# A mixer block on one core: keys and queries in unsplit float32, decay masks on TensorE, gates of both sequences together, and a new order of u, z and Fourier

## The chip, the core and the metric

The program runs on one core of one Trainium2 chip. A core has TensorE (PE; its weight loads are shown as PEld), VectorE (DVE), ScalarE (ACT), GpSimd (POOL) and SyncE (SP), which run side by side; every engine takes its own instructions in the order in which they were written for it. The metric is the device time of the whole program in microseconds; lower is better.

## The reference, cut to what matters

A latent of 256 positions by 1024 channels (`x`) and a context of 256 positions (`ctx`) go through a first block, the mixer, and then through recurrent and feed-forward blocks that the change does not touch. In the first block both sequences are modulated and normalised, projected with `w_in`, and mixed by a gated delta rule in both directions and by a 2-D DFT:

```
p = h @ w_in                                # u 512 | q 512, k 512, v 512 | z 512 | ab 16
qkv = silu(dwconv1d(qkv, conv))             # three taps over positions
q, k = l2norm per head (4 heads of 128)
beta = sigmoid(ab[0:2]);  g = -exp(a_log) * softplus(ab[2:4] + dt_bias)   # 2 directions x 4 heads
gc = cumsum(g);  decay = exp(gc_i - gc_j) where i >= j, else 0
a_mat = strict_lower((k*beta) k^T * decay);  T = inverse(I + a_mat)
S <- S * exp(g_last) + k_dec^T v_new;  o = q_dec S + (q k^T * decay) v_new
y = concat(fourier_mix(u, w_f), rmsnorm(o) * silu(z)) @ w_out
```

The context (called sequence 1 in the kernel) gives only keys, values and gates; its final states start the scan of `x` (sequence 0).

## The kernel before, in words

The change lies in `_block1_mix` and its helpers, the first 275 us of the span. Sequence s has two row tiles t of 128 positions and two directions d.

**Products.** `hT[s]` holds the modulated input, channels on partitions, in float32. A unit of `w_in` (128 x 2048, 1 MB) is loaded by SP into a buffer named raw. For keys and queries both operands are split in a high and a low part in fp32r (`split`: ACT copies the high part, L154, DVE subtracts, L155; names hk, hq, wk), and `cm` (L207) makes 24 fp32r matmuls for one 128 x 256 tile. Values, u and z go through `cmn` and `tmn` (L213, L217): 8 float32 matmuls a tile straight from raw and `hT`, each of which the trace shows as two records. There are 8 key tiles (pk), 4 query tiles (pq), 8 value tiles (pv), and the tiles of u (pu) and z.

**From keys to the inverse.** A key tile goes through the convolution with SiLU (`conv_silu`: L629, L630 and L637 on ACT, L633 to L638 on DVE), is transposed (tk, into kn) and squared (L762). Where all squares are there, POOL takes the power -1/2 (rs, L132) and DVE makes the scalars of `gdn_scalars`. A decay tile is made by `decay`: four small matmuls bring the cumulated gate to PSUM (gr, L941), four DVE instructions subtract the column's own and add a mask of 0 and large negative numbers (L946), one ACT exponential takes all 512 columns (L948). Its results are named E and atT. `Mall` (L784, DVE, 32 instructions of 128 x 128) multiplies key products (kk, L778), a scalar and E. kk and gr tiles share one pool of four PSUM buffers (`PA`). `invert` then inverts 32 x 32 blocks on DVE: four transposes (invB, L1028), a row recurrence (L1038, L1040) with the convolutions of queries and values between its steps, four transposes back (Zall, L1044). The merges follow on PE (zt L1114, y and z L1125), interleaved with the scan (ks, tv, up).

**Work around it.** `fill_step` runs one of 24 dot products on DVE (L258, of 128 x 1024 each) for a modulation vector that later blocks use; its operand is a half unit of `adaT` that POOL's queue loads (nar, L254) into one of two narrow buffers, after an activation and a product on the conditioning row (crow, L236 and L237). Steps are called in the loop over values, held there by `issue_after` until named instructions have been issued, and in the scan. After the scan's first steps come u, the DFT (`fourier`, f L1162) and z as filling, then the output product (bk). The order on each engine is made by a scheduler from this program order and from its estimates; it is fixed before the run.

Of the kernel before, what the change touches and what calls it, by code (L numbers as in the profile page):

```python
# [65 lines left out]
class Program:  # L66
# [67 lines left out]
    def softplus(self, out, in_, n):  # L134

        nc = self.nc
        T = lambda s: self.sm.tile([128, 16], F32, name=self.nm(s), tag=s, bufs=2)[:, :n]
# [504 lines left out]
    def _block1_mix(self, g):  # L642
# [52 lines left out]
        pow_ = self.pow  # L695
        mods = next(mods)
        self.halves()
        del self.scratch
        for s in seqs:
            for k in range(8):  # L700
                A, sh = mods[s]
                if s == 1 and k % 2:
                    nc.scalar.activation(hT[s][k], hT[s][k], AF.Identity, scale=A[:, k:k + 1], bias=sh[:, k:k + 1])
                else:
                    last = nc.vector.tensor_scalar(out=hT[s][k], in0=hT[s][k], scalar1=A[:, k:k + 1], scalar2=sh[:, k:k + 1], op0=ALU.mult, op1=ALU.add)
# [3 lines left out]
        for s in seqs:  # L709
            next(gates[s])  # L710


        four = lambda z: z.rearrange("p (a b) -> p a b", a=4)
        big = T([128, 4, 1024], "hk", "Mall", F32R)
        parts = {1: [four(big[:, i]) for i in range(4)], 0: [T([128, 4, 256], "hq", f"vb{i // 2}{i % 2}", F32R) for i in range(4)]}
        for s in seqs:
            for i in range(2):
                self.split(parts[s][i], parts[s][2 + i], hT[s].tiles[i])
        hp = {s: (Blocks(parts[s][:2]), Blocks(parts[s][2:])) for s in seqs}
# [4 lines left out]
        def split_unit(u, places):  # L724
            w = self.load(a["w_in"][u])
            with ExitStack() as ctx:
                if u >= 4:
                    ctx.enter_context(tc.issue_after(conv.ins))
                for i in range(2):
                    self.split(places[i], places[2 + i], w[:, i * 1024:(i + 1) * 1024])  # L730
            return Weights(places[:2], 256), Weights(places[2:], 256)

        def room(*tags):
            if len(tags) == 1:
                z = T([128, 4, 1024], "wk", tags[0], F32R)
                return [z[:, i] for i in range(4)]
            return [T([128, 1024], "wk", t, F32R) for t in tags]

# [3 lines left out]
        ssq = {s: self.const.tile([128, 2, 4], F32, name=f"ssq{s}") for s in seqs}  # L742
        for u in range(2):
            w = split_unit(u, room("Zall") if u == 0 else room("atT0", "ut", "atT1", "sz"))
            for s in seqs:
                for m in range(2):
                    h = 2 * u + m
                    ps = self.PB("pk")
                    self.cm(ps, w, hp[s], m)
                    conv = self.conv_silu(ps, h, kT[s][:, h])  # L750
                    if (u, s, m) == (0, 1, 1):
                        self.hold = conv
                        gate = {s: next(gates[s]) for s in seqs}
                        scalars = {s: self.gdn_scalars(gate[s], ssq[s], g, s) for s in seqs}
                        gc = {s: next(scalars[s]) for s in seqs}
# [4 lines left out]
                    for t in range(2):  # L760
                        j = self.sm.tile([128, 128], F32, name=self.nm("j"), tag="j", bufs=2)
                        nc.scalar.activation(j, kn[s][:, t, h], AF.Square, accum_out=ssq[s][:, t, h:h + 1])  # L762
                    if u == 1 and early:
                        i = early.popleft()
                        E[i] = self.decay(gate[1][1], gc[1], i[2], i[1], None)
        sc = {s: next(scalars[s]) for s in seqs}
# [6 lines left out]
        for s in seqs:  # L773
            for t in range(2):
# [4 lines left out]
                for d in range(2):  # L779
                    if (s, t, d) not in E:  # L780
                        E[s, t, d] = self.decay(gate[s][1], gc[s], d, t, atT[t][:, d] if s == 0 else None)
# [1037 lines left out]
```

## Time and profile before

| | |
|---|---|
| median of 3 runs | 1677.18 us (1676.41 to 1681.1) |
| profiled execution | 1681.0 us, span 1679.2 us, mean granted clock 0.982 |
| busy in the span | PE 96%, DVE 74%, ACT 51%, POOL 4% |
| first block | up to about 275 us of the span |

The span is what the trace covers; the profiled execution is the slowest of the runs shown. A granted clock of 1.00 is 2.4 GHz and one of 0.50 is 1.2 GHz.

### The profile page before, as it was taken

What the parts mean: (1) busy time and instruction counts of PE and PEld (TensorE: products, weight loads), DVE (VectorE), ACT (ScalarE), POOL (GpSimd) and SP (SyncE); (2) the same over time, 40 slices, a digit from 0 to 9 for tenths busy, and PEclk for the clock granted to TensorE, in tenths of its full rate; (3) what the DMA queues carried; (4) which work ended last, traced back from release to release, by engine and by line L of the source; (5) the groups of instructions that cost most, each with busy time, mean ns of one, the idle gap of its engine ahead of it and who ended that gap; (6) DMA issues with size and microseconds to landing.
All of it is one profiled execution on the core that took longest, in us unless ns stands there. A gap on an engine that the chain in (4) does not pass through costs nothing.

```text
span 1679.2 us, 28977 instructions
## 1 busy us (share of the span) xinstructions
PE 1609.1 (96%) x11712; PEld 1503.4 (90%) x11712; DVE 1246.1 (74%) x2237; ACT 864.1 (51%) x1452; POOL 68.6 (4%) x103
## 2 busy tenths in 40 slices
PE   7969999999969999999999999899999999999998
PEld 2867988899959999999999999799999999999997
DVE  4899666999988784987678667687848876786554
ACT  4725454555546664644446444466646444464443
POOL 1150100000000000000000000000000000000000
PEclk9989999999989999999999999999999999999999
DMA  9332524566765655465665758656554656657552
GB/s 378 117 121 87 170 72 163 180 245 219 272 213 212 209 176 175 149 247 176 225 226 204 261 209 294 237 203 218 176 179 153 239 176 226 226 195 270 176 188 89
DMA packets 51686, 333.86 MB, mean 199 GB/s; under 512 B 6112, under 2 KB 6496, under 8 KB 14688
## 3 DMA queue, kind: packets, MB, share of 16 engines
q1 hardware_dynamic: 47808, 318.38, 53.5%
q0 software_dynamic: 3744, 13.63, 2.5%
q8 instruction: 92, 1.51, 0.4%
q14 instruction: 42, 0.34, 0.1%
HBM read 330.94 MB, written 1.05 MB: 198 GB/s over the span
## 4 chain that ended last, share of the span: by engine, by line
PE 81%; DVE 7%; DMA 5%; issue 4%; ACT 3%; POOL 1%; SPq 0%; DVEq 0%; POOLq 0%; ACTq 0%
PE pj L207 43%; PE bk L1280 12%; PE pj L226 7%; PE pj L496 3%; PE bk L535 2%; DVE wlo L155 1%; DMA raw<-w_in 1%; PE bk L226 1%; PE pu L217 1%; DMA raw<-adaT 1%; ACT whi L154 1%; DMA row<-row 1%; DMA nar<-ada 1%; PE pk L207 1%; PE y L1125 1%
## 5 line engine op out<-in xcount | busy, mean ns | idle before, releaser
L155 DVE TENSOR_TENSOR wlo<-raw,whi 128x1024 fp32r<-128x1024 f32 x438 | 520.7, 1221 | 278.5 <-ACT whi L154 277.8
L154 ACT ACTIVATE whi<-raw 128x1024 fp32r<-128x1024 f32 x438 | 445.7, 1054 | 459.1 <-PE pj L207 302.3
L207 PE MATMUL pj<-hT,whi 128*128 128x256 f32 x3584 | 473.2, 285 | 5.3 <-ACT gac L1238 3.2
L207 PEld LDWEIGHTS pj<-hT,whi 128*128 128x128 f32 x3584 | 450.0, 192 | 9.7 <-ACT gac L1238 3.6
L207 PE MATMUL pj<-hT,wlo 128*128 128x256 f32 x1792 | 252.0, 283 | 0.0
L207 PEld LDWEIGHTS pj<-hT,wlo 128*128 128x128 f32 x1792 | 231.3, 192 | 0.4 <-issue 0.4
L1280 PE MATMUL bk<-whi,hid 128*128 128x512 f32 x688 | 189.1, 397 | 17.0 <-ACT hid L154 17.0
L1280 PEld LDWEIGHTS bk<-whi,hid 128*128 128x128 f32 x688 | 128.5, 191 | 44.1 <-ACT hid L154 18.8
L258 DVE CUSTOM_DVE_ANT_0 raw<-raw,crow 128x1024 f32<-128x1024 f32 x104 | 125.0, 1219 | 12.1 <-DMA raw<-adaT 12.0
L1280 PE MATMUL bk<-wlo,hid 128*128 128x512 f32 x344 | 107.4, 394 | 0.0
L226 PE MATMUL pj<-whi,hT 128*128 128x256 f32 x640 | 84.5, 285 | 0.0
L226 PEld LDWEIGHTS pj<-whi,hT 128*128 128x128 f32 x640 | 80.0, 192 | 0.3
L1280 PEld LDWEIGHTS bk<-wlo,hid 128*128 128x128 f32 x344 | 65.5, 190 | 14.0
L1296 DVE SCALAR_TENSOR_TENSOR gac<-gin,cols,gac 128x189 f32<-128x189 f32 (+2 forms) x176 | 66.1, 426 | 2.2 <-ACT gac L1238 2.1
L496 PE MATMUL pj<-whi,hT 128*128 128x256 f32 x320 | 65.9, 299 | 0.9 <-POOL hT L440 0.4
L496 PEld LDWEIGHTS pj<-whi,hT 128*128 128x128 f32 x320 | 54.3, 203 | 2.7 <-ACT hT L431 1.4
L372 POOL TENSOR_TENSOR ss<-ss,nhalf 128x1 f32<-128x1 f32 x22 | 13.0, 593 | 813.9 <-DVE ss L371 813.9
L226 PE MATMUL pj<-wlo,hT 128*128 128x256 f32 x320 | 44.9, 283 | 0.0
L496 PE MATMUL pj<-wlo,hT 128*128 128x256 f32 x160 | 43.0, 303 | 0.0
L226 PEld LDWEIGHTS pj<-wlo,hT 128*128 128x128 f32 x320 | 41.3, 192 | 0.0
L154 ACT ACTIVATE hid<-r 128x512 fp32r<-128x512 f32 x32 | 20.1, 629 | 35.3 <-DVE r L1330 35.3
L431 ACT ACTIVATE hT<-tp,sh,A 128x128 fp32r<-128x128 f32 x80 | 30.1, 459 | 12.1 <-PE tp L424 9.3
(432 smaller groups left out, 2292.3 us busy)
## 6 DMA issues: line engine op xcount, KB each, us to landing
raw<-w_in SPq DMA_DIRECT2D x98, 1024.0 KB, 4.9
raw<-mlp_w SPq DMA_DIRECT2D x64, 1024.0 KB, 4.9
raw<-adaT SPq DMA_DIRECT2D x52, 1024.0 KB, 5.0
raw<-w_up SPq DMA_DIRECT2D x22, 1024.0 KB, 4.9
nar<-adaT POOLq DMA_DIRECT2D x24, 512.0 KB, 4.2
raw<-w_out SPq DMA_DIRECT2D x12, 1024.0 KB, 4.9
raw<-w_down SPq DMA_DIRECT2D x11, 1024.0 KB, 4.9
raw<-lru_w_o SPq DMA_DIRECT2D x8, 1024.0 KB, 4.8
```

What stands on the lines that cost most here:

```text
L154: self.nc.scalar.activation(hi, v, AF.Copy)
L155: self.nc.vector.tensor_tensor(out=lo, in0=v, in1=hi.bitcast(F32), op=ALU.subtract)
L207: self.nc.tensor.matmul(ps, lhsT=ww[k][:, m * 128:(m + 1) * 128], rhs=xx[k], start=(i == 0 and k == 0), stop=(i == 2 and k == 7))
L217: self.nc.tensor.matmul(ps, lhsT=x[k][:, t * 128:(t + 1) * 128], rhs=w[:, k, :], start=(k == 0), stop=(k == 7))
L226: self.last_product = self.nc.tensor.matmul(ps, lhsT=xx[k][:, t * 128:(t + 1) * 128], rhs=ww[k], start=(i == 0 and k == 0), stop=(i == 2 a ...
L258: nc.vector.tensor_tensor_reduce(out=r, in0=r, in1=self.crow[vec], scale=0.5, scalar=0.0, op0=ALU.mult, op1=ALU.add, accum_out=out[:, k:k ...
L431: q("a", lambda: nc.scalar.activation(H[0][k][:, tk(t)], ps[t, g][:, j], AF.Identity, scale=A[:, k:k + 1], bias=sh[:, k:k + 1]))
L496: self.nc.tensor.matmul(ps[:, t], lhsT=H[lo][k][:, tk], rhs=ww[k], start=(lo == j == i == 0), stop=(lo == 1 and j == 7))
L535: self.nc.tensor.matmul(place(t, n), lhsT=xx[k][:, t * 128:(t + 1) * 128], rhs=ww[k], start=(i == 0 and k == 0), stop=(i == 2 and k == 7))
L1125: mm = lambda ps, l, r: nc.tensor.matmul(ps, lhsT=l, rhs=r, start=True, stop=True)
L1280: self.last_product = self.nc.tensor.matmul(banks[t][h], lhsT=xx[:, k, t * 128:(t + 1) * 128], rhs=ww[k][:, h * 512:(h + 1) * 512], start= ...
L1296: self.nc.vector.scalar_tensor_tensor(out=acc[:, r, c], in0=gin[:, ri, ci], scalar=w, in1=acc[:, r, c], op0=ALU.mult, op1=ALU.add)
```

## The change

Keys and queries are made by `cmn` in float32 from `hT` and raw, without splits. The gates of both sequences are made at once: 32 matmuls with `hT` as weights and 16 columns, one chain of small instructions of 32 columns, one power of 16 columns on POOL. A new function `masks` makes the masks in fp32r once; `decay` starts each of its ten PSUM tiles with one 128 x 512 matmul that puts the mask there, adds the four gate matmuls, and takes four exponentials of 128 x 128 on ACT with the column's own gate as bias. The scan's filling is now all u, then all z, then the DFT, and `fill_step` is called in the loop of u and z and in the scan, with no hold.

```diff
-        gates = {s: self.gates1(wab, hT[s], g, s) for s in seqs}
+        gates = self.gates1(wab, hT, g)
...
-            w = split_unit(u, room("Zall") if u == 0 else room("atT0", "ut", "atT1", "sz"))
+            w = unit(u)
...
-                    self.cm(ps, w, hp[s], m)
+                    self.cmn(ps, w, hT[s], m)
...
-            w = split_unit(4 + u, room("Zall") if u == 0 else room("ut", "b0", "sz", "b1"))
+            w = unit(4 + u)
...
-                self.cm(ps, w, hp[0], m)
+                self.cmn(ps, w, hT[0], m)
...
                     self.cmn(ps, w, hT[s], m)
-                    if m == 0:
-                        with tc.issue_after(last.ins), tc.issue_after(pow_.ins), tc.issue_after(self.hold.ins):
-                            self.fill_step()
...
-            if n == 1:
-                self.fourier(ut, dft, fw[:, 0:2], fw[:, 2:6])
+            self.fill_step()
+        self.fourier(ut, dft, fw[:, 0:2], fw[:, 2:6])
...
+    def masks(self, g):
...
+        for i, (m, sign) in enumerate(((self.ident, 1.0), (self.mup, 1.0), (self.mup, -1.0), (self.mlo, 1.0))):
+            nc.scalar.activation(z[:, i], m, AF.Copy, scale=sign)
+        self.mask = z
...
         def fill(e, mask, sign):
+            gr = self.PA("gr", (128, 4, 128))
+            nc.tensor.matmul(gr, lhsT=self.mask[:, 0], rhs=self.mask[:, mask:mask + 1].to_broadcast([128, 4, 128]), start=True, stop=False)
             for h in range(4):
-                nc.vector.scalar_tensor_tensor(out=e[:, h], in0=gr[:, h], scalar=gc[:, d, t, h:h + 1], in1=mask,
-                                               op0=ALU.subtract, op1=ALU.add if sign > 0 else ALU.subtract)
-            nc.scalar.activation(e, e, AF.Exp, scale=float(sign))
+                nc.tensor.matmul(gr[:, h], lhsT=gg[:, d, h, s, t:t + 1].to_broadcast([128, 128]),
+                                 rhs=self.U if d == 0 else self.L, start=False, stop=h == 3)
+            for h in range(4):
+                nc.scalar.activation(e[:, h], gr[:, h], AF.Exp, scale=float(sign), bias=gc[sign][:, d, h, s, t:t + 1])
             return e
...
+        for s in (1, 0):
+            for t in range(2):
+                for k in range(8):
+                    nc.tensor.matmul(ps[:, s, t], lhsT=hT[s][k][:, t * 128:(t + 1) * 128], rhs=wab[:, k, :], start=(k == 0), stop=(k == 7))
...
-        self.rsqrt(f8(rs), f8(ssq), 8)
+        self.rsqrt(f16(rs), f16(ssq), 16)
```

The two decay tiles that `decay` made from one PSUM tile before now take one each, so ten tiles where there were eight. The scheduler's order changes at three places that matter. The first is PE at the end of the keys and the start of the queries. Before:

```order
L778 MATMUL kk_933<-kT_380 128x128 x3
L941 MATMUL gr_938<-cst,gg_504 128x128 x4
L207 MATMUL pq_1047<-hq_367,wk_1040 128x256 x4
L207 MATMUL pq_1047<-hq_368,wk_1040 128x256 x4
L207 MATMUL pq_1047<-hq_369,wk_1040 128x256 x4
```

Now, where the new line L921 is the mask's matmul and L923 the gate's four:

```order
L752 MATMUL kk_720<-kT_383 128x128 x3
L921 MATMUL gr_725<-masks 128x512
L923 MATMUL gr_725<-cst,gg 128x128 x4
L213 MATMUL pq_839<-hx_221,raw_837 128x256 x3
L921 MATMUL gr_740<-masks 128x512
L923 MATMUL gr_740<-cst,gg 128x128 x4
L213 MATMUL pq_839<-hx_221,raw_837 128x256
L213 MATMUL pq_839<-hx_222,raw_837 128x256
L921 MATMUL gr_750<-masks 128x512
L923 MATMUL gr_750<-cst,gg 128x128 x4
L752 MATMUL kk_764<-kT_383 128x128 x4
```

Three query matmuls stand ahead of gr_740 now, and ahead of it the buffers are taken by kk_694, kk_707, kk_720 and gr_725. The second place is PE where the inverse ends and the merges begin (zt). Before, the last value tiles are followed by 20 matmuls of u, with two transposes (tv) and the query sums (pqs) between them:

```order
L213 MATMUL pv_1472<-hx_222,raw_1386 128x256 x4
L217 MATMUL pu_2223<-raw_2221,hx_221 128x256
L828 MATMUL tv_1465<-cst,vT_1457 128x128 x2
L217 MATMUL pu_2223<-raw_2221,hx_221 128x256 x3
L217 MATMUL pu_2223<-raw_2221,hx_222 128x256 x3
...
L217 MATMUL pu_2245<-raw_2243,hx_221 128x256 x4
L1114 MATMUL zt_1517<-cst,Zall 128x128 x4
L1114 MATMUL zt_1524<-cst,Zall 128x128 x4
L272 MATMUL adr_1639<-cst,gc_1265 128x128
L1125 MATMUL y_1532<-zT_1522,Mall_906 128x128 x4
```

Now the merges follow the last value tile directly, and everything of u stands behind them:

```order
L213 MATMUL pv_1161<-hx_222,raw_1087 128x256 x4
L1091 MATMUL zt_1206<-cst,Zall 128x128 x4
L1091 MATMUL zt_1213<-cst,Zall 128x128 x4
L217 MATMUL pu_1923<-raw_1921,hx_221 128x256 x2
L799 MATMUL tv_1130<-cst,vT_1122 128x128 x2
L1102 MATMUL y_1221<-zT_1211,Mall_693 128x128 x4
L217 MATMUL pu_1923<-raw_1921,hx_221 128x256
L799 MATMUL tv_1154<-cst,vT_1146 128x128 x2
```

In all, 29 matmuls of u, three tv and the pqs stand between the merges up to the scan's fourth step; the rest of u, then z, then the DFT follow. The third place is DVE right behind the inverse's last transposes. Before:

```order
L1044 STREAM_TRANSPOSE Zall<-invX 32x32x32 x4
L131 TENSOR_SCALAR rq_1513<-pqs 128x8
L268 TENSOR_TENSOR gc_1265<-gc_1265,cols 128x8
L258 ISA nar_1802,sh_1247<-nar_1802,crow_1266 128x1024
L258 ISA sh_1247 128x1
L839 TENSOR_SCALAR qs<-qs 128x8
L1119 COPY zc_1529<-Zall 128x512
```

Now three convolutions of values, the product on the conditioning row and the first dots stand there:

```order
L1021 STREAM_TRANSPOSE Zall<-invX 32x32x32 x4
L633 SCALAR_TENSOR_TENSOR vT_1122<-cvx_1123,cwh,vT_1122 128x255
L633 SCALAR_TENSOR_TENSOR vT_1146<-cvx_1147,cwh,vT_1146 128x255
...
L237 SCALAR_TENSOR_TENSOR crow_1329<-nar_1331,crow_1329 128x1024
...
L258 ISA nar_1334,gc_1328<-nar_1334,crow_1329 128x1024
...
L1096 COPY zc_1218<-Zall 128x512
L258 ISA nar_1335,gc_1328<-nar_1335,crow_1329 128x1024
```

All 24 dots stand behind the inverse now; before, 8 stood ahead of it and 16 behind. On ACT, the activation L236 of the conditioning row moved from the twentieth place to the third, ahead of the squares of the context (L339); on POOL the issues of G, crow and the first half unit of `adaT` moved ahead of the first powers (ss, L132).

## Rows read from the trace of the kernel before

**Rows 1.** Windows by stage: length, busy of five engines, PE clock, DMA share, GB/s.
```profile
38.20:80.00 41.80, 40.44 (x293) 34.27 (x294) 36.17 (x119) 30.22 (x85) 2.69 (x5) 0.96 0.41 144
80.00:104.00 24.00, 14.29 (x93) 13.10 (x91) 21.06 (x90) 7.78 (x20) 18.72 (x27) 0.80 0.19 62
112.80:163.00 50.20, 43.73 (x207) 36.02 (x206) 48.23 (x114) 22.34 (x66) 1.64 (x3) 0.97 0.28 94
163.00:249.00 86.00, 84.80 (x688) 75.78 (x689) 54.42 (x144) 41.81 (x119) 11.22 (x17) 1.00 0.38 124
249.00:274.20 25.20, 24.83 (x153) 22.65 (x153) 10.29 (x24) 6.81 (x13) 0.00 (x0) 1.00 0.24 84
```
**Rows 2.** Timeline of PE: start, length, work, idle before, its releaser.
```profile
39.34 8.75 PE L963 MATMUL ab<-hx,wab 128*16 128x256 f32 x32 [1.17 <-issue]
...
77.10 1.19 PE L207 MATMUL pk<-hq,wk 128*128 128x256 f32 x8
...
90.34 1.67 PE L941 MATMUL gr<-cst,gg 128*128 128x128 f32 x8 [2.15 <-DVE Mall L784]
...
104.01 9.61 PE L207 MATMUL pq<-hq,wk 128*128 128x256 f32 x64 [5.72 <-DVE wk L155]
...
154.40 1.95 PE L837 MATMUL pqs<-ones,sq 128*128 128x1 f32 x16
...
163.07 1.06 PE L1114 MATMUL zt<-cst,Zall 128*128 128x128 f32 x8 [2.30 <-DVE Zall L1044]
```
**Rows 3.** Chain of work that ended last: start, length, work.
```profile
48.10 5.97 PE pk L207 x48
...
249.20 13.81 PE pu L217 x64
```
**Rows 4.** Groups by form, 38 to 113 us: count, busy us, mean ns.
```profile
L946 DVE SCALAR_TENSOR_TENSOR E<-gr,gc,cst 128x128 f32<-128x128 f32 x24 | 7.2, 343 | 0.3 <-PE gr L941 0.3
...
L946 DVE SCALAR_TENSOR_TENSOR atT<-gr,gc,cst 128x128 f32<-128x128 f32 x16 | 4.5, 340 | 0.0
```
**Rows 5.** Timeline of ACT, start of the span and first key tile.
```profile
9.80 0.63 ACT L339 ACTIVATE xn<-in_ctx 128x512 f32<-128x512 f32 x1 [7.21 <-DMA in_ctx<-ctx]
...
32.03 1.06 ACT L236 ACTIVATE nar<-crow 128x1024 f32<-128x1024 f32 x1 [4.25 <-DMA crow<-crow]
...
52.05 0.38 ACT L629 ACTIVATE cvx<-pk 128x256 f32<-128x256 f32 x1 [1.56 <-PE pk L207]
...
57.27 0.30 ACT L762 ACTIVATE j<-kn 128x128 f32<-128x128 f32 x1
```
**Rows 6.** Timeline of POOL, whole first block.
```profile
23.20 0.75 POOL L234 DMA_DIRECT2D crow<-crow  x1
...
80.84 2.58 POOL L132 TENSOR_TENSOR rs<-rq,nhalf 128x8 f32<-128x8 f32 x1 [2.32 <-DVE rq L131]
...
164.84 0.69 POOL L254 DMA_DIRECT2D nar<-adaT  x1
...
209.60 0.53 POOL L254 DMA_DIRECT2D nar<-adaT  x1 [2.84 <-DVE A L258]
```
**Rows 7.** Timeline of DVE: products, the inverse's first and last transposes.
```profile
90.31 2.15 DVE L784 SCALAR_TENSOR_TENSOR Mall<-kk,mc,E 128x128 f32<-128x128 f32 x8
...
112.81 2.17 DVE L1028 STREAM_TRANSPOSE invB<-Mall 32x1024 f32<-32x1024 f32 x1
...
154.12 8.81 DVE L1044 STREAM_TRANSPOSE Zall<-invX 32x1024 f32<-32x1024 f32 x4
```
**Rows 8.** A window at the idle before the queries, as Rows 1.
```profile
102.00:104.00 2.00, 0.00 (x0) 0.00 (x0) 2.00 (x6) 0.45 (x1) 0.77 (x2) 0.50 0.10 13
```
**Rows 9.** Groups by form on DVE, 163 to 249 us: busy, mean ns, idle before.
```profile
L258 DVE CUSTOM_DVE_ANT_0 nar<-nar,crow 128x1024 f32<-128x1024 f32 x16 | 19.6, 1222 | 8.9 <-DMA nar<-adaT 8.7
```
**Rows 10.** Timeline of ACT at the end of the first block.
```profile
278.48 0.60 ACT L368 ACTIVATE xn<-bk 128x512 f32<-128x512 f32 x1 [1.69 <-DVE yg L391]
...
279.57 2.01 ACT L154 ACTIVATE whi<-raw 128x1024 fp32r<-128x1024 f32 x2 [0.41 <-DMA raw<-w_up]
```

More of the change, by code (lines that the diff above doesn't have):

```diff
@@ L694, in _block1_mix @@
         self.after = (first,)
-        pow_ = self.pow
         mods = next(mods)
         self.halves()
+        self.masks(g)
         del self.scratch
@@ L704, in _block1_mix @@
                 else:
-                    last = nc.vector.tensor_scalar(out=hT[s][k], in0=hT[s][k], scalar1=A[:, k:k + 1], scalar2=sh[:, k:k + 1], op0=ALU.mult, op1=ALU.add)
+                    nc.vector.tensor_scalar(out=hT[s][k], in0=hT[s][k], scalar1=A[:, k:k + 1], scalar2=sh[:, k:k + 1], op0=ALU.mult, op1=ALU.add)
         wab = T([128, 8, 16], "wab", "wab")
         nc.sync.dma_start(wab, a["w_ab"])
-        gates = {s: self.gates1(wab, hT[s], g, s) for s in seqs}
[L709 to L719, printed above, removed]
+        gates = self.gates1(wab, hT, g)
+        next(gates)
         def unit(u):
             return self.load(a["w_in"][u]).rearrange("p (k n) -> p k n", k=8)
[L724 to L737, printed above, removed]
         E, early = {}, deque((1, t, d) for t in range(2) for d in range(2))
@@ L748, in _block1_mix @@
                     ps = self.PB("pk")
-                    self.cm(ps, w, hp[s], m)
[L750 to L755, printed above, removed]
+                    self.cmn(ps, w, hT[s], m)
+                    self.conv_silu(ps, h, kT[s][:, h])
+                    if (u, s, m) == (0, 1, 0):
+                        gate = next(gates)
+                        scalars = self.gdn_scalars(gate, ssq, g)
+                        gc = next(scalars)
                     pt = self.pst.tile([128, 2, 128], F32, name=self.nm("tk"), tag="pst")
@@ L761, in _block1_mix @@
                         j = self.sm.tile([128, 128], F32, name=self.nm("j"), tag="j", bufs=2)
-                        nc.scalar.activation(j, kn[s][:, t, h], AF.Square, accum_out=ssq[s][:, t, h:h + 1])
+                        nc.scalar.activation(j, kn[s][:, t, h], AF.Square, accum_out=ssq[:, h, s, t:t + 1])
                     if u == 1 and early:
                         i = early.popleft()
-                        E[i] = self.decay(gate[1][1], gc[1], i[2], i[1], None)
-        sc = {s: next(scalars[s]) for s in seqs}
+                        E[i] = self.decay(gate[1], gc, 1, i[2], i[1], None)
+        sc = next(scalars)
         roots = self.pow
@@ L934, in _block1_mix @@
         self.yT = yT
-    def decay(self, gg, gc, d, t, out):
+    def masks(self, g):
         nc = self.nc
-        gr = self.PA("gr", (128, 4, 128))
-        for h in range(4):
-            nc.tensor.matmul(gr[:, h], lhsT=gg[:, d, t, h:h + 1].to_broadcast([128, 128]),
-                             rhs=self.U if d == 0 else self.L, start=True, stop=True)
+        z = g.tile([128, 4, 128], F32R, name="masks")
+        for i, (m, sign) in enumerate(((self.ident, 1.0), (self.mup, 1.0), (self.mup, -1.0), (self.mlo, 1.0))):
+            nc.scalar.activation(z[:, i], m, AF.Copy, scale=sign)
+        self.mask = z
@@ new lines, in gates1 @@
+        fl = lambda z: z.rearrange("p d h s t -> p (d h s t)")
+        xx = self.sm.tile([128, 8, 4], F32, name="xx", tag="xx", bufs=1)
+        nc.vector.tensor_tensor(out=xx, in0=pc[:, 8:16], in1=self.row8[:, 0:8].unsqueeze(2).to_broadcast([128, 8, 4]), op=ALU.add)
+        nc.scalar.activation(by(beta), pc[:, 0:8], AF.Tanh, scale=0.5)
+        self.softplus(fl(gg), xx.rearrange("p a b -> p (a b)"), 32)
+        nea = self.const.tile([128, 8], F32, name="nea")
+        nc.scalar.activation(nea, self.row8[:, 8:16], AF.Exp)
@@ new lines, in gdn_scalars @@
+        mul(by(kd), by(kd), both)
+        nc.vector.scalar_tensor_tensor(out=nrm, in0=f16(ssq), scalar=EPS, in1=f16(rs), op0=ALU.add, op1=ALU.mult)
+        nc.vector.tensor_copy(by(vs)[:, 0], nrm)
+        nc.vector.tensor_copy(by(vs)[:, 1], by(os_)[:, 1])
+        nc.vector.tensor_copy(by(os_)[:, 1], nrm)
+        nc.vector.tensor_scalar(out=by(ks)[:, 0], in0=by(egc)[:, 0], scalar1=-1.0, scalar2=None, op0=ALU.mult)
+        nc.vector.scalar_tensor_tensor(out=by(ks)[:, 1], in0=by(egc)[:, 1], scalar=-1.0, in1=by(m)[:, 1], op0=ALU.mult, op1=ALU.mult)
```

106 lines of the change are left out of this document (44 added, 62 removed).

## The prediction

> **What bounds the kernel now.** First read are the windows by stage, since the change touches only the first 275 us. From 163 us on TensorE is the bound: it works 84.80 of 86.00 us and then 24.83 of 25.20 [rows 1]. Before that it is not: it lacks 24 - 14.29 = 9.7 us from 80 to 104 and 50.2 - 43.73 = 6.5 us from 112.8 to 163, while DVE is busy 21.06 of 24 and 48.23 of 50.2 [rows 1]. There the chain keys, squares, scalars, Mall, inverse, first merge sets the pace, most of it on DVE. The timeline of PE shows where it surfaces: 2.15 us behind Mall, 5.72 us behind the query weights' split, 2.30 us behind Zall [rows 2]. The block's time is thus T0, the start of the first merge (163.07 us), plus the PE work issued behind it: 274.2 - 163.1 = 111.1 us. A gain ahead of T0 counts only if no PE work crosses from before T0 to behind it.
>
> **The prices of the products.** An fp32r matmul with 256 columns takes 5.97 / 48 = 0.124 us, a float32 one 13.81 / 64 = 0.216 us a record and 0.432 us in all [rows 3]. A tile of 24 fp32r matmuls is 2.99 us, one of 8 float32 matmuls 3.45 us; the change adds 0.47 us a tile, 3.7 us on 8 key tiles and 1.9 us on 4 query tiles. In return all splits of these operands leave ACT and DVE, and with them the wait of 5.72 us.
>
> The Trainium skill ("FP8 and Floating Point Precision", section "TensorE Precision Notes") says that true float32 takes four passes through the array, of which the kernel's three split products leave out one. The trace's ratio, 0.432 / 0.124 = 3.5, is below the four of that sentence.
>
> **The change, step by step, on the clock of the profiled execution.**
>
> *Start.* On ACT the activation of the conditioning row now stands ahead of the context's squares, which start at 9.80 us [rows 5]. Its transfer was used 32.03 - 23.20 = 8.8 us after its issue [rows 5, 6]. The issue moves to the front of POOL's queue, behind the clearing of Zall, where I put it at 4.5 us (an estimate); the activation then ends at about 4.5 + 8.8 + 1.1 = 14.4 us and the squares begin 4.6 us later. ACT has 4.25 us of idle time ahead of that same activation alone [rows 5], so most is absorbed. Bounds 0 and +4.6; I take +1.6, nearer to nothing.
>
> *Gates.* 32 float32 matmuls with 16 columns are 64 records; the nearest row, one column wide, gives 1.95 / 16 = 0.122 us each, 7.8 us; 1.5 us more for the half clock that follows an idle PE (0.50 in the idle window shown) [rows 2, 8]. From 39.34 + 1.6 the gates end at 50.2 us (before: 48.1).
>
> *Keys.* Before, the keys run from 48.1 to 77.10 + 1.19 = 78.3 us [rows 2]: 30.2 us, of which 23.9 products and 6.3 others. After: 64 x 0.432 = 27.6 plus 5.1 of others (one set of gate sums falls away), last key at 82.9 us: +4.6.
>
> *Squares and power.* The first key tile goes from ACT's first touch at 52.05 to its second square at 57.6 us, 5.5 us [rows 5], with splits beside it; 5.3 here. POOL's power took 2.58 us for 8 columns [rows 6] and is 16 wide now: at least the 2.6, at most twice that, 5.2; I take 3.0, as most of it should not grow with columns. Scalars at about 91.2 us. Before, half of the products were already done by then, since each sequence had its own power.
>
> *Mall.* 32 products at 2.06 / 8 = 0.257 us [rows 7] are 8.2 us: 99.4 us if the decay tiles are ready. 24 + 16 subtractions of 0.34 us (11.7 us busy) [rows 4] and the queries' splits have left DVE. But the order shows gr_740 behind three key products and gr_725, and the pool has four buffers: gr_740 waits until Mall has read the first (8 products, 93.3 us). PE waits for Mall in the same way now [rows 2]. PE has then only three query matmuls to do, idles some 4 us, and runs on at half clock [rows 8]. What follows goes link by link: a mask and four gate matmuls (eight records 1.67 us [rows 2], with the mask 1.9), four exponentials at 0.30 us [rows 5], four products at 1.0 us. gr_740, then kk_764, then gr_769 and gr_784 each wait for a link; I count 5.1 us beyond the 8.2 (bounds 0 and +7.6). The inverse starts at 104.5 us, before 112.81 [rows 7]: -8.3.
>
> *Inverse.* From 112.81 to 163.07 it is 50.2 us [rows 2, 7]. A dot (1.15 us), some convolutions and small instructions and a wait of 1 us leave it: 47.0. T0 = 151.5 us, 11.5 earlier. The last value tile ends near 142 us (queries and values together are 12 tiles x 3.45 = 41 us of PE from about 101), and PE idles there for up to 10 us, because the order puts the merges straight behind the values.
>
> *Behind T0.* 20 u matmuls (8.64 us), the pqs (1.95 us [rows 2]) and three tv (0.7) cross from before T0 to behind it: 11.3 us. PE was full there, so all of it is added to the 111.1: 122.4. For the half clock after the idle and for places where the chain of merges has less filling I add 2.5 (bounds 0 and +9): 125 us, block products' end at 276.5, +2.3.
>
> *The block's end.* ACT's second square of the output waits behind two splits of 2.01 us [rows 10]; the new order puts both squares first. Bounds 0 and -2.0; I take -1.4.
>
> **Sum.** -11.5 (T0) + 11.3 (work that crosses) + 2.5 - 1.4 = +0.9 us. The profiled execution takes 1681.0 us for a span of 1679.2, 3.8 above the median of 1677.18; the difference is set on the median: 1678 us, no change that can be measured (0.3%, or 5 us, is about what a measurement of this kernel can tell).
>
> **The rivals.**
>
> *Faster.* The decay tiles do not hold Mall (-5.1) and the start hides its squares (-1.6): 0.9 - 6.7 = -5.8, 1671 us; with nothing lost in the merges as well 1669. For it: ACT does exponentials of 0.30 us quickly, and DVE is free at that time. Against it: four buffers and a fixed PE order; 2.15 us of such a wait stand in the trace already [rows 2]. Chance 0.27.
>
> *Slower.* The dots become a wait. All 24 stand behind the inverse, with two narrow buffers; 15 loads issued from 164.84 to 209.60 us make one each 3.2 us [rows 6], and DVE idled 8.7 us for 16 of them [rows 9]. For 24 this makes 13 us of idle DVE, in which the residuals (r) and states (S) of the scan are queued behind the waiting dot, and PE behind them. Before, PE lost only 1.2 us of 86 [rows 1], since u and the DFT lay between the merges; if two thirds of the 13 us surface, +8: 1686 us. It decides as soon as a load lasts longer than the DVE work between two dots. Chance 0.22.
>
> *Dearer float32.* Were a float32 matmul worth four fp32r ones, 0.498 us in place of 0.432, 64 of them would make the last key 4.2 us later, and T0 and the end with it: 1682 us. The rows at 0.432 are of the same instruction, on the same operands' kinds, so chance 0.05. It is what the four passes of the Trainium skill ("FP8 and Floating Point Precision") would give.
>
> **How the numbers follow.** The forecast holds 0.46, the faster rival 0.27, the slower ones 0.27. The range goes from 1667 (the faster case with its bounds) to 1688 (the dots with a start that is 2 us later); the likeliest case's own range is 1673 to 1682.
>
> **What the profile after would show.** Right, if key and query matmuls are 0.43 us, the last key ends near 83 us, invB starts near 104 with PE idle for Mall ahead of it, zt starts near 151 behind an idle PE of up to 10 us, and the products behind it take 125 us to the output product's first half. Wrong, if invB starts before 100 (the buffers did not hold), if zt to bk is well over 125 us with DVE idle for nar (the dots), if the powers on POOL grow with columns to 5 us, or if the start shows hx later by several us.

## The result and the profile after

The changed kernel takes 1696.26 us (median of 4 runs, 1691.7 to 1700.54) against 1678.61 us for the kernel before: ratio 1.0097, 95% interval 1.0077 to 1.0118. It is slower by about 16 us, which lies outside the predicted range. The profiled execution takes 1697.21 us with a span of 1695.4, 16.2 us above that of before.

First, where the span grew. The chain of work of the changed kernel (start, length, work), from the start to the inverse; `...` marks rows left out:

```profile
5.08 9.72 DMA crow<-crow
14.83 1.06 ACT nar L236
15.88 2.45 ACT xn L339 x8
...
44.34 1.82 PE ab L943 x14
46.16 1.04 PE pk L213 x2
47.20 5.36 PE ab L943 x26
...
56.58 3.65 PE ab L943 x18
60.24 6.65 PE pk L213 x24
...
89.97 2.16 PE pk L213 x10
...
93.87 0.39 ACT cvx L629
...
98.73 2.92 POOL rs L132
...
102.58 2.07 DVE Mall L758 x8
104.69 0.50 PE gr L921
...
111.26 2.16 DVE invB L1005
```

The row's activation stands ahead of the context's squares, which begin at 15.8 us instead of 9.80 [rows 5]; the gates start at 44.34 instead of 39.34 [rows 2], and take until 60.24. Float32 products cost what was predicted, 2.16 / 10 = 0.216 us a record, and the 16 wide power 2.92 us (predicted 3.0). The hold of gr_740 is there too (PE idle for Mall 2.12 us, ahead of 104.69), but the inverse starts only 8.8 us after Mall begins, not 13.3. The timeline of DVE shows why: while gr_740 was made, eight more products were ready, and DVE ran 16 without a gap.

```profile
102.49 4.21 DVE L758 SCALAR_TENSOR_TENSOR Mall<-kk,mc,E 128x128 f32<-128x128 f32 x16
...
108.97 1.12 DVE L758 SCALAR_TENSOR_TENSOR Mall<-kk,mc,atT 128x128 f32<-128x128 f32 x4 [0.21 <-ACT atT L926]
```

The windows of the changed kernel through the gates and the first keys (columns as in [rows 1]):

```profile
44.00:46.00 2.00, 1.66 (x15) 1.69 (x15) 2.00 (x7) 1.71 (x4) 0.00 (x0) 0.95 0.69 291
46.00:48.00 2.00, 2.00 (x9) 1.82 (x9) 1.46 (x5) 0.00 (x0) 0.00 (x0) 0.50 0.00 0
...
58.00:60.00 2.00, 2.00 (x11) 2.00 (x10) 0.00 (x0) 0.00 (x0) 0.00 (x0) 0.50 0.00 0
60.00:62.00 2.00, 2.00 (x7) 1.64 (x7) 1.61 (x12) 0.53 (x3) 0.00 (x0) 0.50 0.00 0
62.00:64.00 2.00, 2.00 (x9) 1.69 (x8) 1.26 (x14) 0.52 (x2) 0.00 (x0) 0.79 0.00 0
```

PE is busy all the time, and yet its clock stays at 0.50 (1.2 GHz) from 46 to 62 us. It rises at about 63 us, in the key products behind the last of the gates. In the kernel before it was low at this place too, but only for some 3 us, behind a PE that had idled, and it rose under the gates themselves:

```profile
38.00:40.00 2.00, 0.83 (x6) 0.41 (x6) 1.54 (x7) 1.21 (x4) 0.00 (x0) 0.91 1.02 430
40.00:42.00 2.00, 2.00 (x6) 0.66 (x5) 2.00 (x7) 2.00 (x5) 0.00 (x0) 0.50 0.87 360
42.00:44.00 2.00, 2.00 (x8) 0.84 (x7) 2.00 (x5) 1.89 (x2) 0.00 (x0) 0.74 0.19 78
44.00:46.00 2.00, 2.00 (x11) 0.88 (x10) 2.00 (x2) 0.89 (x2) 0.00 (x0) 1.00 0.00 0
```

Behind the inverse, the timeline of PE (idle before, and its releaser, in brackets):

```profile
159.42 1.94 PE L1091 MATMUL zt<-cst,Zall 128*128 128x128 f32 x8 [3.52 <-DVE Zall L1021]
...
250.06 0.49 PE L845 MATMUL o<-vx,atT 128*128 128x128 f32 x2 [1.72 <-DVE atT L837]
...
253.87 6.49 PE L217 MATMUL pu<-raw,hx 128*128 128x256 f32 x21 [2.03 <-DVE sz L874]
```

and the timelines of ACT and DVE there:

```profile
246.29 2.00 ACT L154 ACTIVATE wm<-raw 128x1024 fp32r<-128x1024 f32 x2 [6.50 <-DMA raw<-w_out]
```
```profile
247.38 2.36 DVE L155 TENSOR_TENSOR wm<-raw,wm 128x1024 fp32r<-128x1024 f32 x2 [2.61 <-ACT wm L154]
249.66 0.35 DVE L837 SCALAR_TENSOR_TENSOR atT<-qk,rs,atT 128x128 f32<-128x128 f32 x1
249.92 1.22 DVE L258 CUSTOM_DVE_ANT_0 nar<-nar,crow 128x1024 f32<-128x1024 f32 x1
...
251.06 1.22 DVE L258 CUSTOM_DVE_ANT_0 nar<-nar,crow 128x1024 f32<-128x1024 f32 x1
...
252.21 1.28 DVE L847 TENSOR_TENSOR os<-o,os 128x512 f32<-128x512 f32 x2
253.41 0.74 DVE L874 SCALAR_TENSOR_TENSOR sz<-sz,pu 128x256 f32<-128x256 f32 x2
```

The first merge starts at 159.42, only 3.7 us before that of [rows 2]. From there to the second half of the output product (first L226 matmul, 274.23 before, 290.80 now) it is 131.4 us instead of 111.2. Of the 20.2 us more, 12.1 are work, 4.5 clock loss and 3.6 idle time. Two waits make most of the 5.1 us that PE idles there now. It waits 1.72 us for the last atT, which stands behind the output weights' split: u, which comes later, holds its buffer longer, so that load is issued at 239.4 us instead of 205.0, and ACT's split waits 6.50 us for it. It then waits 2.03 us for sz, which stands on DVE behind two dots and os.

One count serves all that follows. From the gates' first matmul to the output product's second half, in windows of 2 us, the last one cut short, PE's idle time is the length less its busy time, its clock loss is busy time times (1 - granted clock), and the rest is work at full clock. Before: 234.9 us = 18.0 idle + 8.0 clock + 208.9 work. After: 246.5 = 15.1 + 13.0 + 218.4. With 5.0 us from the later start the block ends 16.6 us later: +5.0 start, +9.5 work, +5.0 clock, -2.9 idle.

### The profile page after: what moved, and what is told of

Its sections match the earlier page's. It is cut to its first block, busy times and chain, and to the rows that moved or that the text cites. A ratio compares the mean times of both kernels' runs of the same rounds, so it can differ in the third digit from the quotient of the medians.

```text
span 1695.4 us, 28812 instructions
## 1 busy us (share of the span) xinstructions
PE 1627.2 (96%) x11664; PEld 1515.1 (89%) x11664; DVE 1223.3 (72%) x2145; ACT 860.2 (51%) x1467; POOL 66.3 (4%) x102
## 4 chain that ended last, share of the span: by engine, by line
PE 81%; DVE 9%; DMA 4%; ACT 3%; issue 1%; POOL 1%; DVEq 0%; POOLq 0%; ACTq 0%
PE pj L207 41%; PE bk L1257 11%; PE pj L226 7%; PE pj L496 3%; DVE wlo L155 2%; PE bk L535 2%; DMA raw<-adaT 2%; PE pu L217 1%; PE bk L226 1%; PE pk L213 1%; DMA raw<-w_in 1%; PE fr L590 1%; DVE raw L258 1%; DVE gac L1273 1%; PE y L1102 1%
## 5 line engine op out<-in xcount | busy, mean ns | idle before, releaser
L1257 PE MATMUL bk<-whi,hid 128*128 128x512 f32 x688 | 189.1, 396 | 18.4 <-ACT hid L154 18.4
L226 PE MATMUL pj<-whi,hT 128*128 128x256 f32 x640 | 84.5, 285 | 0.0
L226 PEld LDWEIGHTS pj<-whi,hT 128*128 128x128 f32 x640 | 80.0, 192 | 0.3
L226 PE MATMUL pj<-wlo,hT 128*128 128x256 f32 x320 | 44.9, 283 | 0.0
L372 POOL TENSOR_TENSOR ss<-ss,nhalf 128x1 f32<-128x1 f32 x22 | 12.1, 551 | 820.3 <-DVE ss L371 820.3
L226 PEld LDWEIGHTS pj<-wlo,hT 128*128 128x128 f32 x320 | 41.3, 192 | 0.0
L258 DVE CUSTOM_DVE_ANT_0 nar<-nar,crow 128x1024 f32<-128x1024 f32 x24 | 29.0, 1219 | 14.9 <-DMA nar<-adaT 14.8
```

Source lines behind the costliest of these rows:

```text
L226: self.last_product = self.nc.tensor.matmul(ps, lhsT=xx[k][:, t * 128:(t + 1) * 128], rhs=ww[k], start=(i == 0 and k == 0), stop=(i == 2 a ...
L258: nc.vector.tensor_tensor_reduce(out=r, in0=r, in1=self.crow[vec], scale=0.5, scalar=0.0, op0=ALU.mult, op1=ALU.add, accum_out=out[:, k:k ...
L1257: self.last_product = self.nc.tensor.matmul(banks[t][h], lhsT=xx[:, k, t * 128:(t + 1) * 128], rhs=ww[k][:, h * 512:(h + 1) * 512], start= ...
```

## The experiments

The stages of one profiled execution each, in us. The columns are: start of the gates' first matmul, end of the last key product, start of the inverse's first transposes, start of the first merge (zt), start of the output product's second half, then the three parts of the count above, and the time (median of all executions, or the only one where marked 1; for the kernel before, of the 20 that ran beside the last experiments). What each run is stands with it below.

| run | gates | last key | inverse | first merge | second half | idle | clock | work | time |
|---|---|---|---|---|---|---|---|---|---|
| before | 39.34 | 78.29 | 112.81 | 163.07 | 274.23 | 18.0 | 8.0 | 208.9 | 1679.23 |
| after | 44.34 | 93.84 | 111.26 | 159.42 | 290.80 | 15.1 | 13.0 | 218.4 | 1696.26 |
| late_row | 38.52 | 86.39 | 103.85 | 152.02 | 282.66 | 14.6 | 11.0 | 218.5 | 1683.86 (1) |
| wide_gates | 43.67 | 85.74 | 103.17 | 152.87 | 285.96 | 14.7 | 8.5 | 219.2 | 1691.46 (1) |
| dft_mid | 44.28 | 95.22 | 114.26 | 163.97 | 299.54 | 17.5 | 20.7 | 217.1 | 1708.26 (1) |
| f32_only | 38.41 | 88.84 | 113.80 | 167.71 | 278.55 | 16.9 | 8.7 | 214.6 | 1686.57 |
| u_ahead | 44.68 | 94.18 | 111.60 | 172.39 | 292.44 | 16.8 | 11.6 | 219.3 | 1702.20 (1) |
| dots_early | 38.65 | 94.09 | 113.31 | 161.50 | 290.62 | 16.1 | 18.4 | 217.5 | 1699.58 (1) |
| late_wide | 38.27 | 80.33 | 97.79 | 147.49 | 280.29 | 14.5 | 8.5 | 218.8 | 1685.90 |
| late_wide_u | 38.50 | 80.57 | 99.66 | 160.50 | 280.04 | 16.6 | 4.8 | 220.2 | 1686.24 |
| late_wide_split | 38.77 | 75.52 | 101.26 | 151.70 | 281.84 | 22.8 | 7.2 | 213.1 | 1686.94 (1) |
| late_wide_dve | 39.04 | 81.85 | 106.16 | 160.31 | 286.65 | 21.1 | 10.0 | 216.5 | 1697.65 (1) |
| joint_only | 39.33 | 78.15 | 108.10 | 160.62 | 271.37 | 16.2 | 7.5 | 208.3 | 1675.69 |
| joint_masks | 38.59 | 76.81 | 105.33 | 154.33 | 274.01 | 17.1 | 6.5 | 211.8 | 1681.71 |
| order_dots | 37.97 | 74.70 | 101.73 | 150.63 | 273.26 | 16.7 | 6.2 | 212.4 | 1682.42 |
| order_dft | 38.01 | 76.37 | 103.41 | 152.39 | 269.74 | 15.7 | 3.1 | 213.0 | 1681.66 |
| joint_masks_f32 | 38.39 | 84.62 | 103.78 | 153.45 | 288.47 | 19.7 | 12.6 | 217.8 | 1694.16 |

Ratios to before, with intervals: f32_only 1.0035 (1.0017 to 1.0053), late_wide 1.0039 (1.0019 to 1.0059), late_wide_u 1.0038 (1.0022 to 1.0054), joint_only 0.9965 (0.9941 to 0.9989), joint_masks 1.0004 (0.9987 to 1.002), order_dots 1.0015 (0.9999 to 1.003), order_dft 1.0015 (0.9993 to 1.0037), joint_masks_f32 1.0082 (1.0055 to 1.0109). Times of one kernel spread by up to 14 us (order_dft 1673.68 to 1687.73, its profiled run is the lowest), so a stage counts below where its mechanism is seen, and a total where an interval stands. One thing must be kept apart: in the profiled executions of wide_gates, late_wide, dots_early and joint_masks_f32 a stretch of some 10 us behind the first merge runs at 0.50 with PE busy all the time, which costs 5.1 us in each. The changed kernel and late_row, which have the same work there, don't show it. So a difference of 5 us of clock between two single executions behind the merge says nothing of an edit.

**The start.** late_row holds POOL's issues back:

```diff
-                with tc.issue_after(self.turned_back.ins):
+                with tc.issue_after(self.turned_back.ins), tc.issue_after(pow_.ins):
                     self.fill_step()
```

> One edit to the changed kernel: POOL's issues of the conditioning row, of G and of the first half unit of adaT wait again until POOL's powers for both sequences have been issued, as before the change; the activation of the row then stands behind the squares on ACT. Start theory (the activation of the row, which waits for its transfer until 14.8 us, holds up the context's squares and all that hangs on them): squares begin near 9.8 us, the gates' first matmul starts near 39.5 us instead of 44.34, and the block's end (last output product's first half, 290.8 us) comes 4 to 5 us earlier. Rival (the start is late because of something else in the change, such as the masks' copies on ACT or their matmuls on PE): squares at 9.8 us but gates still near 44 us.

The squares begin at 9.89 us and the gates at 38.52 us, 5.8 earlier, and the block ends 8.1 us earlier: the start theory holds, though the masks' copies and matmuls stay. Some 2 of the 8.1 us are a smaller clock loss (11.0 against 13.0), which the edit doesn't explain.

**The gates.** wide_gates makes the products in the old form and transposes them:

```diff
-                    nc.tensor.matmul(ps[:, s, t], lhsT=hT[s][k][:, t * 128:(t + 1) * 128], rhs=wab[:, k, :], start=(k == 0), stop=(k == 7))
+                nc.tensor.matmul(pa, lhsT=wab[:, k, :], rhs=hT[s][k], start=(k == 0), stop=(k == 7))
```

> One edit to the changed kernel: the gates' products are made in the form of before (the 16 gate columns as weights, 256 positions as moving columns, then four small transposes), all else of the change kept. Form theory (PE's clock stays at half speed through the gates because of the form of these matmuls): from the gates' first matmul the clock is back at 1.00 within some 4 us, as before the change, the gates take about 9 us, the last key ends 6 to 7 us earlier (87 instead of 93.8 us), and the block's end comes some 6 us earlier. Rival (the clock stays low for about 17 us after the idle start whatever runs): the clock stays at 0.50 until about 62 us and the last key moves by less than 2 us.

The windows of wide_gates at the same place:

```profile
46.00:48.00 2.00, 2.00 (x11) 0.88 (x10) 1.13 (x4) 0.24 (x1) 0.00 (x0) 1.00 0.00 0
...
58.00:60.00 2.00, 2.00 (x11) 1.75 (x10) 2.00 (x18) 0.89 (x2) 0.00 (x0) 1.00 0.00 0
```

The clock is 1.00 throughout; gates and keys take 42.1 us (43.67 to 85.74) instead of 49.5. The form theory holds, in its size too (7.4 us), though the block's end comes 4.8 us earlier, not 6. That 42.1 is near the 42.0 of the prediction is luck: this run has no clock loss there, where the prediction counted 1.5 us, and 1.0 us more work than the changed kernel (41.7 against 40.7).

The other runs agree. Five executions have the form with 16 moving columns (the changed kernel, late_row, dft_mid, u_ahead, dots_early), and each loses 6.8 to 10.2 us of clock from the gates to the last key. The twelve with the old form lose 0 to 1.7 us, but for 4.9 in f32_only, where PE stood idle for 3.2 us among the keys. What in the new form keeps the clock low no run separates.

**Two orders behind the inverse.** dft_mid puts the DFT back between u and z; u_ahead writes u's first unit ahead of the merges:

```diff
+        for n in range(1):
+            w = unit(6 + n)
...
         merges = [self.merge(
```

> One edit to the changed kernel: the DFT is put back between u and z. Order theory (with the DFT last, its four groups stand at the end of the block with nothing between their links but the output product, and PE waits some 5 us for z's and the DFT's results from 249 to 282 us): the end of the output product's first half comes 4 to 6 us earlier than 290.8, PE's idle time behind the scan falls below 2 us. Rival (the time behind the first merge is work and half clock, not order): the end moves by less than 1.5 us.

> One edit to the changed kernel: the first unit of u (16 matmuls, 6.9 us) is written ahead of the merges, and with it the last three transposes of values and the query sums stand there again; start and gates as in the change. Order theory (PE idles 3.5 us ahead of the first merge, runs the next 6 us at half clock, and the buffers of u come free late, so that the output weights' load is late and PE idles again from 246 to 254 us): from the first merge to the output product's second half 120 to 124 us instead of 131.4, PE's idle plus half-clock loss behind the first merge 3 us or less instead of 9.6, the first merge 3 to 6 us later than 159.4, block end 286 us or earlier (was 290.8). Rival (the work only moves across the first merge, nothing is saved): block end within 1.5 us of 290.8.

Both theories fell. dft_mid ends 8.7 us later than the changed kernel; 4.5 of these lie ahead of the first merge, with 5.1 us more clock loss there, so that only 4.2 us can be the order's. Behind the merge it has 7.5 us of idle PE instead of 5.1 and 7.0 us of clock loss instead of 4.5 (one execution each). In u_ahead the merge moves from 159.42 to 172.39 and the stretch behind it from 131.4 to 120.0: the work only changed sides (the end, 292.44, is 1.6 us later, where the rival allowed 1.5). Its transposes of the last values wait for convolutions that DVE does behind the inverse's last transposes, and u stands behind them on PE (4.91 us idle at that place in late_wide_u).

u_ahead also shows that the late load of the output weights was not what its order theory took it for. The load is issued at 227.26 us here, and ACT waits 0.80 us for it; yet PE idles as long behind the merge as in the changed kernel (5.6 against 5.1 us), and for the same results (timelines of ACT and PE):

```profile
234.07 2.00 ACT L154 ACTIVATE wm<-raw 128x1024 fp32r<-128x1024 f32 x2 [0.80 <-DMA raw<-w_out]
```
```profile
249.81 0.49 PE L853 MATMUL o<-vx,atT 128*128 128x128 f32 x2 [2.54 <-DVE atT L845]
```

On DVE two dots (one with 1.59 us of waiting for its operand), a split and os stand one behind the other ahead of atT.

**The dots.**

> The changed kernel with the dots' steps back in the loop over values, with the hold of before: 8 dots stand ahead of the inverse again, 16 behind it, and the conditioning row is late again as in the run late_row. Dots theory (24 dots behind the inverse make DVE wait for their loads, 14.8 us in the changed kernel, and PE behind it): the stretch from the first merge to the output product's second half gets 4 us or more shorter than the 130.6 us of late_row. Rival (the waits of DVE for the loads are hidden behind PE, which was full from 166 to 246 us): that stretch stays within 2 us of 130.6, and the dots ahead of the inverse only make the first merge later.

129.1 us against 130.6: by the length the rival holds, but the parts say something else. PE's idle time behind the merge falls from 4.6 to 1.4 us, and PE waits neither for atT nor for sz. The four profiled kernels that differ from each other only in start and gates and have all 24 dots behind the inverse (after, late_row, wide_gates, late_wide) idle 4.4 to 5.1 us there. So these waits go with the dots' place; in this order the split of the output weights also stands behind atT on DVE. The gain is lost to the clock (6.6 us of loss instead of 4.2), of which 5.1 are the stretch at 0.50 described above, which late_row doesn't have. The run as a whole is slower than late_row (1699.58 against 1683.86): its first merge comes 9.5 us later, as the rival said of the dots ahead of the inverse; 4.8 of these are idle time and 4.9 clock loss.

In the changed kernel DVE does wait, as this row of its waits from 158 to 300 us says (total, times, longest):

```profile
DVE nar L258 <- DMA nar<-adaT: 14.8, 8, 3.9
```

All eight waits fall between 165 and 246 us, where PE was full; what reached PE came behind them, where dots stood ahead of sz.

**What is left without start and gates.**

> Two edits to the changed kernel: the conditioning row late (as late_row) and the gates' products in the form of before (as wide_gates). If the two effects are independent (5.3 us at the gates' start, 7.4 us from the gates' start to the last key), the last key ends near 80.5 us, the first merge starts near 147 us, the output product's second half near 278 us, and the time is 12 to 13 us below the changed kernel: 1683 to 1685 us, still 3 to 6 us over the kernel before, which is then the loss of the order behind the inverse alone. If one hides the other: 1687 us or more.

> The two edits of late_wide and the first unit of u ahead of the merges (as u_ahead). If the three effects together are the whole loss of the change: the output product's second half starts near 269 to 272 us, before the 274.2 of the kernel before, and the time is 1673 to 1677 us, below the kernel before. If the order of u saves nothing, as late_wide: 1683 to 1685 us.

late_wide takes 1685.9 us: the two mishaps, start and gates, were 10 us of the loss, and independent up to the last key (80.33) and the first merge (147.49). The second half came 2 us later than expected, at 280.29 (with the 5.1 us stretch at half clock in it), and u ahead of the merges (late_wide_u, 1686.24 us) again saves nothing. PE has 9.9 us more work than before.

**One part at a time.** f32_only removes the splits from the kernel before and nothing else:

> One part of the change alone, on the kernel before: keys and queries in float32 without splits; gates, decay, dots and the order of u, DFT, z as before. If the float32 products themselves are the loss (the part that adds PE work: 0.47 us on each of 12 tiles, 5.6 us), 1681 to 1685 us. If the freed DVE and ACT are worth more than that (the inverse starts earlier and u is still put ahead of the merges), 1668 to 1676 us, and the loss of the whole change lies in the other parts.

1686.57 us, ratio 1.0035: slower than before, about the 5.7 us by which its PE work is larger. late_wide_split and late_wide_dve undo one part of late_wide:

> The kernel of late_wide with keys and queries made from split fp32r operands again, as before the change; joint gates, masks on PE and the new order stay. Work theory (in a block in which PE idles little, its work at full clock sets the length: late_wide has 218.8 us of it from the gates to the output product's second half, the kernel before 208.9, the float32 products alone 214.6): 213 us of PE work, the output product's second half at 274 to 276 us instead of 280.3. Rival (the splits' DVE and ACT work, 19 us of DVE, comes back on the path to the inverse and eats the PE time saved): first merge 5 us or more later than 147.5 and the output product's second half at 279 us or later.

> The kernel of late_wide with the decay tiles made as before the change: eight PSUM tiles, subtraction and mask on DVE, one exponential of 512 columns; no mask matmuls. Work theory: PE work falls by the masks and the two extra tiles, about 4 us, and as PE is the bound behind the first merge the output product's second half comes 1 to 4 us earlier than 280.3, though the first merge comes later. Rival (the 11.7 us of DVE work that the masks take off the way to the inverse are worth more than 4 us of PE): first merge 5 us or more later, output product's second half 2 us or more later.

Neither theory of late_wide_split holds alone: PE work is 213.1 us, as expected, and the first merge only 4.2 us later, but idle rises by 8.3 us, most of it behind the merge, and nothing is gained. Its PE and DVE timelines show why:

```profile
237.94 0.80 PE L869 MATMUL o<-vx,atT 128*128 128x128 f32 x2 [6.16 <-DVE atT L861]
...
246.62 0.70 PE L217 MATMUL pu<-raw,hx 128*128 128x256 f32 x2 [2.69 <-DVE sz L898]
```
```profile
229.68 1.23 DVE L258 CUSTOM_DVE_ANT_0 nar<-nar,crow 128x1024 f32<-128x1024 f32 x1 [2.80 <-DMA nar<-adaT]
...
235.25 1.22 DVE L258 CUSTOM_DVE_ANT_0 nar<-nar,crow 128x1024 f32<-128x1024 f32 x1
...
236.39 1.22 DVE L258 CUSTOM_DVE_ANT_0 nar<-nar,crow 128x1024 f32<-128x1024 f32 x1
...
237.54 4.22 DVE L861 SCALAR_TENSOR_TENSOR atT<-qk,rs,atT 128x128 f32<-128x128 f32 x16
```

Here PE has run out of other work, and three dots, a wait for the first one's load, a split of the output weights and os stand ahead of atT. In late_wide_dve the decay on DVE makes the first merge 12.8 us later and saves 2.3 us of PE work, and the second half comes 6.4 us later: the rival holds.

joint_only and joint_masks build up from the kernel before:

> The kernel before with one part of the change alone, the gates and scalars of both sequences in one chain (one softplus of 32 columns, one power of 16), their matmuls in the form of before; splits, decay on DVE, dots and the order as before. The joint chain takes small DVE instructions away but lets all Mall products wait for the squares of both sequences. If the saved instructions matter: 1674 to 1678 us. If the wait for both sequences' squares costs as much: 1679 to 1683 us, no change.

> joint_only with the decay masks on PE as in the change (ten tiles, four exponentials each): what is left of the change without the float32 products, without the new gate matmuls and without the new order of dots, u, z and DFT. If the masks' 11.7 us off DVE bring the inverse forward and PE takes 4 us more work: first merge 4 to 8 us earlier than 163, time 1674 to 1679 us, at or a little below the kernel before. If PE's added work counts in full: 1683 us or more.

joint_only takes 1675.69 us, ratio 0.9965: by 0.35% faster than the kernel before, clear of noise, and faster than the changed one. All Mall products wait for one power, and the inverse still starts at 108.10 instead of 112.81. With masks (joint_masks) the first merge is another 6.3 us earlier, PE has 3.5 us more work, and the time, 1681.71 us, is that of before and lies between the two expectations: the gain ahead of the merge is paid back behind it.

**The order again, and float32 under the old order.** Of the 16.6 us by which the change ends the block later, the step from joint_masks to late_wide_split (the new order of dots, u, z and DFT; 274.01 to 281.84, one execution each) holds 7.8 us. The next two runs ask which half of that order loses them.

> joint_masks (output product's second half at 274.0 us) with only the dots moved as in the change: none ahead of the inverse, all 24 behind it, steps called in the loop of u and z; the DFT stays between u and z. Dots theory (the dots and the waits for their loads stand in DVE's queue ahead of the scan's and the attention's instructions, and PE waits for those): most of the 7.8 us, 279 to 283 us, with PE idle for atT. Rival (the DFT behind z is the loss): 273 to 276 us.

> joint_masks with only the DFT moved behind z as in the change; 8 dots ahead of the inverse and 16 in the scan as before. Dots theory: 273 to 276 us. Rival (the four groups of the DFT at the block's end have nothing to hide behind, and z's products wait for their PSUM readers): 279 to 283 us.

> joint_masks with keys and queries in float32 straight from the loaded unit, as in the change; dots, u, DFT and z in the order of before. Work theory (5.7 us more PE work in a block that PE fills): output product's second half 3 to 6 us later than 274.0, time 1683 to 1687 us. Rival (the splits freed from ACT and DVE pay for it): 272 to 275 us, time 1678 to 1682 us.

Each half alone costs nothing that is measured (1.0015 each, against 1.0004 for joint_masks). Both theories expected one half to carry the 7.8 us, and neither does. Only both together make the 6.16 us wait shown in late_wide_split, of which there is one execution; that they need each other is inferred from these three. Float32 in place of the splits costs 12 us under the old order (1694.16 against 1681.71). In the two profiled executions it is 14.7 us: +6.0 work, +6.1 clock, +2.6 idle, with u pushed behind the first merge; 5.1 of the clock are the stretch at 0.50, which the execution of joint_masks doesn't have. Under the new order float32 shows no cost (late_wide against late_wide_split, of which there is one execution): +5.7 work, -8.3 idle, +1.3 clock. Under float32 the new order even looks better than the old one (late_wide 1685.90 against 1694.16). The parts do not add.

## Why the prediction was wrong, step by step

*Start.* "Bounds 0 and +4.6; I take +1.6, nearer to nothing" failed: it cost 5.0 us, nearly the whole delay of the squares (15.8 against 9.8 us is 6.0). ACT's idle time of 4.25 us did not absorb it, because it lay behind the squares and not ahead of them: in the chain of the changed kernel the squares are followed almost without a gap by work of ACT and PE up to the gates. late_row gives 5.8 us back.

*Gates.* "1.5 us more for the half clock that follows an idle PE" failed. The prediction took the clock as an after-effect of idle time; it stayed at 0.50 for 16 us of busy PE and cost 8.5 us up to the last key. From the gates' first matmul to the last key it was 49.5 us instead of 42.0, with 40.7 us of work, where the prediction has 40.5; wide_gates shows that the clock is the whole difference.

*Keys, squares, power.* Right in time: 0.216 us a record, power 2.92, first Mall 8.7 us after the last key (predicted 8.3). The power was right by luck. The prediction priced 8 columns at 2.58 us and let little of it grow; the second power of 8 columns in the same trace of before takes 1.67,

```profile
87.16 1.67 POOL L132 TENSOR_TENSOR rs<-rq,nhalf 128x8 f32<-128x8 f32 x1 [3.19 <-DVE rq L131]
```

so that 8 columns more cost some 1.25 us. The Trainium skill ("FP8 and Floating Point Precision", section "TensorE Precision Notes") counts four passes for true float32; by the trace a float32 matmul costs 3.5 fp32r ones, so that rival fell.

*Mall.* gr_740 was held as predicted, but DVE was not: 8.8 us from the first Mall to the inverse, predicted 13.3. PE idled 2.12 us and not 4, its clock was still 1.00 there, and the link's mask, gate and exponential ran beside eight products that were ready, so that DVE idled 0.21 us. *Inverse.* 48.2 us to the first merge, predicted 47.0; PE idles 3.52 us ahead of it, not up to 10. T0 thus came at 159.42, predicted 151.5: +3.4 start, +7.5 gates, +0.4 power, -4.5 Mall, +1.2 inverse.

*Behind T0.* The crossing work was right: 121.8 us of work against 109.7, 12.1 more (predicted 11.3). The 2.5 us for half clock and thinner filling was mis-sized: idle and clock loss went from 1.5 to 9.6 us, 8.1 more, within its upper bound of 9. Of the 9.6, 2.9 are half clock behind the idle ahead of the first merge, 5.3 the waits for atT and sz and the half clock at that place, and the rest is mostly in the DFT's links.

*The block's end.* -1.4 predicted; from the second half to the next block's first product 14.05 us instead of 14.72, -0.7.

*The sum.* +0.9 predicted; T0 came 7.9 us later than predicted, the stretch behind it was 6.4 us longer, and the end 0.7 us dearer: 15.9, where the span grew by 16.2.

*The rivals.* The slower side came, but the dots are the smaller part of it. DVE's wait for their loads was predicted well (13 us, 14.8 measured); what surfaced on PE was not 8 us but 3.3 of idle time, by dots_early. It surfaces where PE has nothing else to do, as in late_wide_split. The faster rival's premise (Mall hardly held) came true and was buried. The range failed because three terms missed on the slow side at once: the start went past its bound of 4.6, the gates' clock had no bound, and the term behind T0 came near its bound of 9. The range's ends had been set by one rival at a time.

## What to carry to other kernels

Count PE's work at full clock, idle and clock loss apart, over the stretch in which it is the bound: a change that adds work to PE to relieve another engine pays only as long as it removes as much idle time. Look at where an instruction without a hold floats to in each queue, and what waits behind it, before pricing it by its length. When an operand pair changes roles in a matmul (weights for moving columns), do not carry the old clock over. And before a difference of a few microseconds between two traces is put down to an edit, look whether one of them has a stretch at half clock that the other lacks.

## What the hardware showed that I had not expected

The granted clock fell to 0.50 and stayed there for 16 us while PE's busy share was 2.00 of 2.00, as long as the matmuls were mainly those with 16 moving columns. The same products with 256 columns ran at 1.00 in wide_gates, and in the kernel before a clock of 0.50 was back at 1.00 after some 3 us of them.

It fell once more with PE full, for some 10 us, in late_wide (162 to 172 us):

```profile
162.00:164.00 2.00, 2.00 (x13) 1.88 (x13) 1.27 (x5) 0.40 (x2) 0.59 (x1) 0.50 0.06 23
...
168.00:170.00 2.00, 2.00 (x18) 1.79 (x18) 1.04 (x2) 0.38 (x1) 0.00 (x0) 0.50 0.00 0
```

It stood behind the query sums (one column) and the merges' products of 64 columns. wide_gates, dots_early and joint_masks_f32 show the same stretch at that work, 5.1 us of loss each, and dft_mid one of 3.4; in the changed kernel and in late_row the same work in the same place ran at 1.00. So that work alone does not decide it, and what does stays open. Total clock loss in one traced execution of these kernels ranges from 3.1 to 20.7 us.

A power on POOL grew with its columns: 0.55 us for 1, 1.02 for 4, 1.67 for 8 (in the kernel before) and 2.92 for 16 (in the changed one), all on 128 partitions.
